# Turning the maxima of a unit as f16, in the step and the bank of the sums

## The chip, the cores and the metric

The kernel runs on one core of one Trainium2 chip. The metric is the device time of one launch in microseconds (us). A core has TensorE (PE; weight loads are shown as PEld), VectorE (DVE), ScalarE (ACT), GpSimd (POOL) and SyncE (SP, which issues most DMAs here). The time before is 2743.02 us, the median of three runs from 2740.77 to 2745.37.

## What is computed

One layer of a bidirectional encoder on two sequences of 2048 tokens, each token 1024 wide, with the same weights. Cut to what matters here:

```python
u = rmsnorm(h, g_norm)
q, k, v, ga, f, gf = split(u @ w_in)              # 8 q heads, 2 kv heads of 64; gates; Fourier input
q, k = rope(rmsnorm(q, g_q)), rope(rmsnorm(k, g_k))
s  = einsum('bkgqd,bskd->bkgqs', qblk, k) * 64 ** -0.5      # 128 queries at a time
pr = softmax(s, axis=-1)
a  = einsum('bkgqs,bskd->bqkgd', pr, v) * silu(ga)
fo = real(fft2(f)) @ w_fmix * silu(gf)
h  = h + concat([a, fo]) @ w_out
h  = h + (p @ w_ple) * sigmoid(rmsnorm(h, g_ple) @ w_ple_gate)
y  = rmsnorm(h, g_final)
```

The change concerns the softmax alone: the maximum of each query's scores, which is taken off before the exponential.

## The kernel before

The program has three stretches. The first, to about 844 us, projects both sequences (`project`). The second, to about 2668 us, is attention; between its steps one filling generator puts work of the other branch into the same engines' queues: first the Fourier branch (`fourier2`), then the output projections (`outp`). What is left of the filling work runs last.

**Units and steps.** Attention has 64 units; a unit is a sequence, a kv head and 128 queries of that head's four q heads. Step `g` belongs to unit `u = g // 8` and block `j = g % 8` of its keys. In a step `scores(u, j)` (L1141) multiplies two half-arrays of keys by the queries into two banks of `ps_s`, ScalarE takes the exponentials `p` (L1144), and GpSimd adds them up into `acc` (L1147, L1149, L1151). The score products stand transposed, keys on partitions, queries along columns. In steps 0 and 4 ("heavy" ones) TensorE multiplies four blocks of `p` by V (`pv`, L1205) and no filling work follows; in the other steps `interleave` draws some, by shares that are fixed in the program.

**Maxima.** A query's maximum has to be known before its first exponential, so each unit's scores are computed once more ahead of time, with queries on partitions: `lead(g)` runs eight pieces `maxima(v, k)` (L1168, two half-array f16 products into the only buffer of `ps_m`, and a row maximum on VectorE, L1176), `AHEAD` = 13 steps before `g`. After the last piece L1181 makes `m4`, [128 queries, 4 heads]. `negate` (L1186, ScalarE) writes it, negated and scaled by 2^-12, twice into a zeroed f32 tile `nm` of 128 x 128. `max_rows` (L1191) turns it: a product with the identity puts the queries along the columns, into 128 columns of a bank of PSUM. L1193 (VectorE) multiplies that by `own`, which leaves each head's row at its place, and writes the f16 tile `mr`; the first product of the next unit's step 0 adds `mr` to the scores with the weights `kone` (2^12).

**The order around it.** PE, ACT, DVE and SP work in the order in which the program issues. With `AHEAD` = 13 and `g = 8u + j`, the last piece of unit u+1 comes in step j = 2, the first of unit u+2 in j = 3, `negate(u+1)` in j = 4 and `max_rows(u+1)` in j = 6, behind that step's maxima. In step 4 `sums(u-1)` (L1237) multiplies `acc` by ones into 256 columns of a bank and `divide` (L1244, L1245, VectorE) takes the reciprocal in place and scales unit u-1's output. `run_slow` then issues one of the long second halves of a split (L1383, L1527) or a final scaling (L1513), two of them in step 0. `load_q` (L1127) loads the queries of unit u+2 at j = 0.

**Banks.** `bank()` gives out banks of PSUM: during the Fourier branch in turn from `ps_g` (two) and `ps_f` (one); once the output projection has begun (`self.grouped`), from the one bank of `ps_f` alone. It is asked for the turn, for the sums and for the embedding products of the filling work (L445 into `ps_f`, read by L1421 and L1423 on VectorE).

**The first unit.** Before attention there are no steps: `leads()` runs the first 13 pieces of `lead` inside the projection's sweeps, one at a time, with the two-bank form of `maxima` in `ps_x`, and `max_rows(0)` behind the piece of g = -2. What is left of them is drained near the end of the projection (L823).

Of the kernel before, what the change touches and what calls it, by code (L numbers as in the profile page):

```python
# [10 lines left out]
F32 = mybir.dt.float32  # L11
F16 = mybir.dt.float16
I32 = mybir.dt.int32
AF = mybir.ActivationFunctionType
ALU = mybir.AluOpType
# [13 lines left out]

CAP = 5.0  # L30
FILL = 765.0
AHEAD = 13
PVG = 4
NBF = 5
NW = 16
# [105 lines left out]
class Build:  # L141
# [957 lines left out]
    def attention(self, kvp):  # L1099
# [3 lines left out]
        nc, st = self.nc, self.st  # L1103
        units = self.unit_order()
        n = len(units)
# [82 lines left out]

        def max_rows(u, ps):

            nc.tensor.matmul(ps, nm[:], self.ident[:], start=True, stop=True)  # L1191
            MR[u] = mr = kvp.tile([128, 4, 128], F16, name="mr", bufs=1)
            nc.vector.tensor_tensor(out=mr[:], in0=ps.unsqueeze(1).to_broadcast([128, 4, 128]),  # L1193
                                    in1=own[:].unsqueeze(2).to_broadcast([128, 4, 128]), op=ALU.mult)

        def pv(u, j0):
            s, kv, t = units[u]
# [56 lines left out]
        for kv in range(2):  # L1254
            load_kv(0, kv)
            load_q(kv)
        nm = kvp.tile([128, 128], F32, name="nm", bufs=1)
        nc.gpsimd.memset(nm[:], 0.0)
        kone = kvp.tile([128, 128], F16, name="kone", bufs=1)
        nc.gpsimd.memset(kone[:], K_ONE)  # L1260
# [11 lines left out]
        def leads():  # L1272
            for g in range(-AHEAD, 0):
                yield from lead(g)
                yield
                if g == -2:
                    max_rows(0, self.bank()[:, 0:128])

        self.ahead = leads()
        pool = yield 0.0  # L1280
# [3 lines left out]
        for g in range(8 * n + 7):  # L1284
            self.step = g
            self.flush()
            u, j = g // 8, g % 8
            if j == 0 and 0 <= u and u + 2 < n:
                load_q(u + 2)
            if j == 4 and u - 1 in fresh:  # L1290
                load_kv(1, fresh[u - 1])
            if 0 <= u < n:
                scores(u, j)
            self.drain(lead(g))
            if j == 4 and 0 <= u - 1 < n:
                ps = self.bank()
                sums(u - 1, ps[:, 0:256])
                divide(u - 1, ps[:, 0:256])
            heavy = (g - 1) % PVG == PVG - 1 and 0 <= g - 1 < 8 * n
            if heavy:  # L1300
                self.run_slow(2 if j == 0 else 1)
                pv((g - 1) // 8, (g - 1) % 8 - PVG + 1)
            if j == 6 and u + 1 < n:
                max_rows(u + 1, self.bank()[:, 0:128])
            yield 0 if heavy else RATE if g >= 8 * n // 2 else 1 if g > FIRST else SLOW


# [547 lines left out]
```

## Time and profile before

| | |
|---|---|
| runs, median | 2743.02 us |
| profiled execution | 2747.83 us, span 2746.0 us |
| granted TensorE clock, mean | 0.991 |
| PE busy | 2649.2 us (96%) |
| DVE busy | 1702.8 us (62%) |
| POOL busy | 1631.3 us (59%) |
| ACT busy | 1213.0 us (44%) |
| DMA | 296.73 MB, mean 108 GB/s |

The profiled execution is one run with the profiler on; its rows carry all durations below. The span runs from the first to the last instruction. Busy times overlap, and a product's duration on PE holds its way through the array, so products that follow each other overlap too: what a product costs the queue is read from the distance between the starts of its neighbours. In rows of products "64\*128" or "128\*128" is the used part of the array (rows \* columns), and an f32 product shows as two rows.

### The profile page before, as it was taken

The numbers are of one execution on the slowest core, as the hardware profiler recorded it, in microseconds if no ns is written. First come the engines' busy times: TensorE is split into PE (matmuls) and PEld (weight loads), VectorE is DVE, ScalarE is ACT, GpSimd is POOL, SyncE is SP. The second block draws the span as 40 slices with busy tenths as digits, with TensorE's granted clock in tenths as the row PEclk, the third lists the DMA queues.
The fourth block names the chain that finished last, engine by engine and source line by source line (L and its number), as shares of the span: only waits on it lengthen the run. The fifth ranks groups of instructions, "written<-read, shape, count | busy, mean of one in ns | idle before, by whom it ended". The sixth has DMA issues, their size and how long they took to land.

```text
span 2746.0 us, 46196 instructions
## 1 busy us (share of the span) xinstructions
PE 2649.2 (96%) x18176; PEld 1261.7 (46%) x18176; DVE 1702.8 (62%) x2477; ACT 1213.0 (44%) x2047; POOL 1631.3 (59%) x1394
## 2 busy tenths in 40 slices
PE   6899999999998998999999999999999999999998
PEld 3455565655555553444434444344444334444443
DVE  6755555564455775666666666666666667666644
ACT  3434333342224553454544555445545445444442
POOL 1223323242335886777777777777777777777760
PEclk9999999999999999999999999999999999999999
DMA  7567567675427662122222223322222222222223
GB/s 233 144 177 199 163 192 189 180 189 118 140 71 229 215 215 83 45 60 63 74 61 60 55 67 81 88 63 69 56 79 58 64 70 68 58 72 74 58 68 76
DMA packets 418554, 296.73 MB, mean 108 GB/s; under 512 B 259456, under 2 KB 360000, under 8 KB 418336
## 3 DMA queue, kind: packets, MB, share of 16 engines
q1 hardware_dynamic: 405424, 252.01, 35.0%
q0 software_dynamic: 12912, 41.77, 4.2%
q8 instruction: 142, 2.33, 0.4%
q14 instruction: 76, 0.62, 0.1%
HBM read 149.50 MB, written 86.51 MB: 86 GB/s over the span
## 4 chain that ended last, share of the span: by engine, by line
PE 86%; DVE 6%; issue 2%; DMA 2%; ACT 1%; POOL 1%; SPq 0%; DVEq 0%; ACTq 0%; POOLq 0%
PE ps_g L1473 22%; PE ps_o L1205 16%; PE ps_x L445 15%; PE ps_s L1141 13%; PE ps_f L445 6%; PE ps_g L445 6%; PE ps_m L1168 4%; PE ps_f L1237 1%; DVE a_mx L1176 1%; PE ps_f L1191 1%; PE ps_g L1012 1%; PE ps_g L1060 1%; DVE w_mx L312 1%; ACT p L1144 0%; PE ps_x L911 0%
## 5 line engine op out<-in xcount | busy, mean ns | idle before, releaser
L1149 POOL TENSOR_TENSOR acc<-acc,p 128x1024 f32<-128x1024 f32 x384 | 910.7, 2372 | 217.8 <-ACT p L1144 172.7
L1176 DVE TENSOR_REDUCE a_mx<-ps_m 128x1 f32<-128x1024 f32 x499 | 610.1, 1223 | 529.9 <-PE ps_m L1168 520.8
L1144 ACT ACTIVATE p<-ps_s,s_scale 128x512 f32<-128x512 f32 x1024 | 647.2, 683 | 659.1 <-PE ps_s L1141 645.6
L1473 PE MATMUL ps_g<-w_pg,hT 64*128 64x512 f16 x2784 | 494.8, 377 | 5.8 <-DMA hT<-h_hl 5.7
L1205 PE MATMUL ps_o<-p,v 128*64 128x512 f32 x2048 | 466.1, 597 | 0.0
L445 PEld LDWEIGHTS <-uc 128*128 128x128 f16 x3072 | 301.3, 98 | 311.8 <-issue 22.4
L1141 PE MATMUL ps_s<-q,k 64*128 64x512 f16 x3072 | 435.0, 378 | 4.9 <-ACT p L1144 4.8
L1473 PEld LDWEIGHTS <-hT 64*128 64x128 f16 x2784 | 200.2, 94 | 165.3 <-issue 20.7
L1141 PEld LDWEIGHTS <-k 64*128 64x128 f16 x3072 | 149.6, 94 | 250.8 <-issue 128.0
L1473 PE MATMUL ps_g<-w_wo,mh 64*128 64x512 f16 x1440 | 261.6, 378 | 1.4 <-DVE seen L1439 1.4
L1205 PEld LDWEIGHTS ps_o<-p,v 128*64 128x64 f32 x2048 | 141.7, 137 | 257.3 <-issue 248.2
L1473 PE MATMUL ps_g<-w_wo,mT 64*128 64x512 f16 x1440 | 256.7, 377 | 0.6 <-DMA mT<-mh 0.6
L1168 PE MATMUL ps_m<-k,q 64*128 64x512 f16 x998 | 202.3, 377 | 11.4 <-DVE a_mx L1176 9.6
L1147 POOL TENSOR_TENSOR acc<-p,p 128x1024 f32<-128x1024 f32 x64 | 150.7, 2354 | 97.7 <-ACT p L1144 97.0
L445 PEld LDWEIGHTS <-w_ga 128*128 128x128 f16 x1536 | 151.4, 99 | 53.7 <-issue 23.3
L928 POOL DMA_DIRECT2D gfd<-gt x32 | 19.2, 601 | 216.0 <-DVE gt L956 211.1
L1473 PEld LDWEIGHTS <-mh 64*128 64x128 f16 x1440 | 99.3, 94 | 89.6 <-issue 14.5
L1473 PEld LDWEIGHTS <-mT 64*128 64x128 f16 x1440 | 100.6, 94 | 84.6 <-issue 2.3
L1221 ACT ACTIVATE tb<-ps_o,a_scale 64x256 f32<-64x256 f32 x128 | 60.0, 469 | 167.4 <-PE ps_o L1205 166.6
L445 PE MATMUL ps_x<-uc,w_ga 128*128 128x256 f16 x1008 | 115.8, 276 | 6.8 <-ACT ge L913 6.2
L1244 DVE RECIPROCAL ps_f<-ps_f 128x256 f32<-128x256 f32 x61 | 107.1, 1756 | 14.2 <-PE ps_f L1237 14.2
L946 POOL DMA_DIRECT2D agd<-gat x64 | 35.8, 559 | 134.7 <-DVE gat L956 134.5
(331 smaller groups left out, 3404.2 us busy)
## 6 DMA issues: line engine op xcount, KB each, us to landing
q<-qTd SPq DMA_DIRECT2D x256, 64.0 KB, 2.2
ag<-agd SPq DMA_DIRECT2D x64, 256.0 KB, 3.3
out<-h POOLq DMA_DIRECT2D x31, 512.0 KB, 3.0
x<-in_x_prompt SPq DMA_DIRECT2D x16, 512.0 KB, 5.6
w_st<-in_w_out SPq DMA_DIRECT2D x32, 256.0 KB, 4.3
gfd<-gt POOLq DMA_DIRECT2D x32, 256.0 KB, 3.2
gd<-ge POOLq DMA_DIRECT2D x32, 256.0 KB, 3.6
agd<-gat POOLq DMA_DIRECT2D x64, 128.0 KB, 2.4
```

Source lines behind the costliest of these rows:

```text
L445: self.nc.tensor.matmul(ps, lhs(ia, k), rhs(ib, k), start=(i == 0), stop=(i == 3 * ks - 1))
L946: nc.gpsimd.dma_start(self.agd[s][1, r * 128:(r + 1) * 128, c * n:(c + 1) * n], gt[:, :n])
L1141: nc.tensor.matmul(S[u][e][:], w[sl], q[sl].rearrange("p h q -> p (h q)"), start=j == i == 0, stop=i + 1 == len(todo), skip_group_check=True)
L1144: nc.scalar.activation(p[:, e, :], S[u][e][:], AF.Exp, scale=self.sc["s_scale"][:])
L1147: nc.gpsimd.tensor_tensor(out=ACC[u][:], in0=P[u, 0][:], in1=p[:], op=ALU.add)
L1149: nc.gpsimd.tensor_tensor(out=ACC[u][:], in0=ACC[u][:], in1=p[:], op=ALU.add)
L1168: nc.tensor.matmul(ps[c], Q[u][0][sl, h, :], kt[s, kv, half][sl, :, 0, :], start=True, stop=True)
L1176: nc.vector.reduce_max(MX[u][:, h, half, c:c + 1], x, axis=AX.X)
L1205: nc.tensor.matmul(o[64 * e:64 * e + 64, :], vt[s, kv, c // 8][:, c % 8, :], p[:, e, :], start=(j == 0), stop=(j == 7))
L1221: nc.scalar.activation(tb[64 * e:64 * e + 64], ov[64 - 64 * e:128 - 64 * e, e], AF.Copy, scale=self.sc["a_scale"][64 - 64 * e:128 - 64 * e ...
L1244: nc.vector.reciprocal(r, r)
L1473: nc.tensor.matmul(g[0][:], g[1](ia, k)[sl], g[2](ib, k)[sl], start=a, stop=z, skip_group_check=True)
```

## The change

`AHEAD` goes from 13 to 14: each piece of maxima and each `negate` comes one step sooner, so the last piece of unit u+1 is in j = 1, the first of unit u+2 in j = 2 and `negate(u+1)` in j = 3. `nm` becomes an f16 tile, and the identity is copied once into an f16 tile `id16` on GpSimd, so the turn is an f16 product. It leaves step 6 and is issued in step 4 ahead of the sums, into columns 256 to 383 of the bank that the sums take anyway; the multiplication into `mr` follows behind `divide`. `max_rows` returns this multiplication as a function for that purpose. Of the pieces that run inside the projection there is one more.

```diff
-AHEAD = 13
+AHEAD = 14
...
         def max_rows(u, ps):
 
-            nc.tensor.matmul(ps, nm[:], self.ident[:], start=True, stop=True)
+            nc.tensor.matmul(ps, nm[:], id16[:], start=True, stop=True)
             MR[u] = mr = kvp.tile([128, 4, 128], F16, name="mr", bufs=1)
-            nc.vector.tensor_tensor(out=mr[:], in0=ps.unsqueeze(1).to_broadcast([128, 4, 128]),
-                                    in1=own[:].unsqueeze(2).to_broadcast([128, 4, 128]), op=ALU.mult)
+            return lambda: nc.vector.tensor_tensor(out=mr[:], in0=ps.unsqueeze(1).to_broadcast([128, 4, 128]),
+                                                   in1=own[:].unsqueeze(2).to_broadcast([128, 4, 128]), op=ALU.mult)
...
-        nm = kvp.tile([128, 128], F32, name="nm", bufs=1)
+        id16 = kvp.tile([128, 128], F16, name="id16", bufs=1)
+        nc.gpsimd.tensor_copy(id16[:], self.ident[:])
+        nm = kvp.tile([128, 128], F16, name="nm", bufs=1)
...
                 if g == -2:
-                    max_rows(0, self.bank()[:, 0:128])
+                    max_rows(0, self.bank()[:, 0:128])()
...
-            if j == 4 and 0 <= u - 1 < n:
+            if j == 4:
                 ps = self.bank()
-                sums(u - 1, ps[:, 0:256])
-                divide(u - 1, ps[:, 0:256])
+                if u + 1 < n:
+                    turned = max_rows(u + 1, ps[:, 256:384])
+                if u > 0:
+                    sums(u - 1, ps[:, 0:256])
+                    divide(u - 1, ps[:, 0:256])
+                if u + 1 < n:
+                    turned()
             heavy = (g - 1) % PVG == PVG - 1 and 0 <= g - 1 < 8 * n
             if heavy:
-                self.run_slow(2 if j == 0 else 1)
+                self.run_slow(1 if j else 2)
                 pv((g - 1) // 8, (g - 1) % 8 - PVG + 1)
-            if j == 6 and u + 1 < n:
-                max_rows(u + 1, self.bank()[:, 0:128])
```

On TensorE, before, a step 6 in the middle of the program; q and k are tiles of queries and keys, hT and mT the operands of the filling work (in such listings an f32 product is one row and has no row for its weight load):

```order
L1141 MATMUL ps_s<-q_16740,k_7187 128x512
L1168 LDWEIGHTS q_17320
L1168 MATMUL ps_m<-k_17145,q_17320 128x512
L1168 LDWEIGHTS q_17320
L1168 MATMUL ps_m<-k_17145,q_17320 128x512
L1191 MATMUL ps_f<-ident,nm 128x128
L1473 LDWEIGHTS mT
L1473 MATMUL ps_g<-w_wo_8663,mT 128x512
L1473 LDWEIGHTS hT
L1473 MATMUL ps_g<-w_pg_9864,hT 128x512
```

There the turn stands between half-array maxima and half-array filling work. On TensorE, now, a step 4 in the middle of the program:

```order
L1141 MATMUL ps_s<-q_16721,k_7187 128x512
L1168 LDWEIGHTS q_17299
L1168 MATMUL ps_m<-k_17123,q_17299 128x512
L1168 LDWEIGHTS q_17299
L1168 MATMUL ps_m<-k_17123,q_17299 128x512
L1191 LDWEIGHTS nm
L1191 MATMUL ps_f<-id_7200,nm 128x128
L1237 MATMUL ps_f<-acc,ones 64x256 x2
L1205 MATMUL ps_o<-p_17305,v_7190 64x512 x2
```

The turn, with a weight load of its own as f16, has moved between the maxima and the sums. On VectorE, before, from the end of a step 3 (the eviction L1421, L1423 of an embedding product) to step 6; L1527 is the second half of a split:

```order
L1421 SCALAR_TENSOR_TENSOR ps_f<-th,ps_f 128x512
L1423 SCALAR_TENSOR_TENSOR h<-ps_f,p_wp_6899,h 128x512
L1176 TENSOR_REDUCE a_mx<-ps_m 128x1 x2
L1244 RECIPROCAL ps_f<-ps_f 128x256
L1245 TENSOR_TENSOR at<-at,ps_f 128x256
L1527 SCALAR_TENSOR_TENSOR h_hl<-h,h_r,h_hl 128x1024
L1176 TENSOR_REDUCE a_mx<-ps_m 128x1 x2
L1193 TENSOR_TENSOR mr<-ps_f,own 128x512
L1176 TENSOR_REDUCE a_mx<-ps_m 128x1
```

Now, the same place (line numbers behind L1258 are up to five higher: L1426, L1428 and L1532 are L1421, L1423 and L1527 of before):

```order
L1426 SCALAR_TENSOR_TENSOR ps_f<-th,ps_f 128x512
L1428 SCALAR_TENSOR_TENSOR h<-ps_f,p_wp_6899,h 128x512
L1176 TENSOR_REDUCE a_mx<-ps_m 128x1 x2
L1244 RECIPROCAL ps_f<-ps_f 128x256
L1245 TENSOR_TENSOR at<-at,ps_f 128x256
L1193 TENSOR_TENSOR mr<-ps_f,own 128x512
L1532 SCALAR_TENSOR_TENSOR h_hl<-h,h_r,h_hl 128x1024
L1176 TENSOR_REDUCE a_mx<-ps_m 128x1 x3
```

The multiplication has moved from behind step 6's maximum to ahead of the split's second half and of step 5's maximum. The other instructions of TensorE, VectorE and ScalarE keep their order, and SP's is unchanged.

## Rows read from the trace of the kernel before

**Rows 1.** The page of the profile: busy time of each engine with its share of the span and its instructions; then the chain of work that ended last, as shares of the span by engine.

```profile
PE 2649.2 (96%) x18176; PEld 1261.7 (46%) x18176; DVE 1702.8 (62%) x2477; ACT 1213.0 (44%) x2047; POOL 1631.3 (59%) x1394
...
PE 86%; DVE 6%; issue 2%; DMA 2%; ACT 1%; POOL 1%; SPq 0%; DVEq 0%; ACTq 0%; POOLq 0%
```

**Rows 2.** Busy time in two windows of the span (window and its length; busy us of PE, PEld, DVE, ACT and POOL, each with its count; granted clock; DMA share; GB/s).

```profile
857.00:1110.00 253.00, 238.48 (x1656) 128.24 (x1658) 162.81 (x199) 128.72 (x213) 189.06 (x134) 0.96 0.57 181
1110.00:2668.00 1558.00, 1539.53 (x11470) 634.67 (x11468) 1004.24 (x1030) 768.11 (x1278) 1161.53 (x969) 1.00 0.25 66
```

**Rows 3.** All of TensorE's waits from 1110 to 2668 us (who waited for whom: us in total, times, longest).

```profile
PE ps_m L1168 <- DVE a_mx L1176: 6.1, 9, 1.2
PE ps_f L445 <- DVE mr L1193: 6.0, 5, 1.5
PE ps_f L1191 <- DVE h L1423: 4.0, 6, 0.7
PE ps_s L1141 <- ACT p L1144: 2.0, 9, 0.3
```

**Rows 4.** The turn's line from 1110 to 2668 us on PE: duration in ns (min/median/max), first and last start.

```profile
L1191 PE MATMUL ps_f<-ident,nm x110: 275/326/377, 1116.5 to 2626.9; 128*128 128x128 f32 x110
```

**Rows 5.** TensorE in order of time (start us, length us, engine, line, operation, out<-in, count): first the maxima and the filling work of a step 5, then the scores, maxima, turn and filling work of the step 6 behind it.

```profile
1712.06 0.38 PE L1168 MATMUL ps_m<-k,q 64*128 64x512 f16 x2
1712.28 0.38 PE L1473 MATMUL ps_g<-w_wo,mh 64*128 64x512 f16 x1
...
1714.22 0.81 PE L1141 MATMUL ps_s<-q,k 64*128 64x512 f16 x6
1714.87 0.38 PE L1168 MATMUL ps_m<-k,q 64*128 64x512 f16 x2
1715.18 0.49 PE L1191 MATMUL ps_f<-ident,nm 128*128 128x128 f32 x2
1715.60 0.39 PE L1473 MATMUL ps_g<-w_wo,mT 64*128 64x512 f16 x1
```

**Rows 6.** TensorE, a step 6 in which the turn waited for its bank (in brackets the idle time and what ended it).

```profile
1553.45 0.38 PE L1168 MATMUL ps_m<-k,q 64*128 64x512 f16 x2
1554.50 0.49 PE L1191 MATMUL ps_f<-ident,nm 128*128 128x128 f32 x2 [0.67 <-DVE h L1423]
1554.92 1.47 PE L1473 MATMUL ps_g<-w_wo,mT 64*128 64x512 f16 x12
```

**Rows 7.** TensorE beside the Fourier branch: maxima and the next product in a step 6, with its turn between them (not shown), and in the step 7 behind it, without one.

```profile
874.73 0.38 PE L1168 MATMUL ps_m<-k,q 64*128 64x512 f16 x2
...
875.36 1.06 PE L1012 MATMUL ps_g<-bd,fT 128*128 128x128 f32 x8
...
877.91 0.38 PE L1168 MATMUL ps_m<-k,q 64*128 64x512 f16 x2
878.22 1.16 PE L1012 MATMUL ps_f<-bd,fT 128*128 128x128 f32 x8
```

**Rows 8.** TensorE, the step 4 of the same unit: maxima and sums.

```profile
1707.05 0.40 PE L1168 MATMUL ps_m<-k,q 64*128 64x512 f16 x2
1707.39 0.65 PE L1237 MATMUL ps_f<-acc,ones 128*64 128x256 f32 x4
```

**Rows 9.** TensorE in the projection: 24 f16 products of 256 columns in the full array, and what follows them.

```profile
808.82 2.78 PE L445 MATMUL ps_x<-wr_kv,uc 128*128 128x256 f16 x24
811.43 0.81 PE L445 MATMUL ps_x<-w_f,uc 128*128 128x512 f16 x3
```

**Rows 10.** VectorE in that unit: the second half of a split behind the reciprocal of step 4, the maximum of step 5, and the multiplication of step 6.

```profile
1710.76 1.70 DVE L1527 SCALAR_TENSOR_TENSOR h_hl<-h,h_r,h_hl 128x1024 f16<-128x1024 f32 x1
1712.49 1.22 DVE L1176 TENSOR_REDUCE a_mx<-ps_m 128x1 f32<-128x1024 f32 x1
...
1716.43 0.68 DVE L1193 TENSOR_TENSOR mr<-ps_f,own 128x512 f16<-128x512 f32 x1
```

**Rows 11.** The closest place: VectorE's maximum of a step 5, and TensorE's maxima of the step 6 behind it.

```profile
1739.90 1.21 DVE L1176 TENSOR_REDUCE a_mx<-ps_m 128x1 f32<-128x1024 f32 x1
...
1741.47 0.57 PE L1168 MATMUL ps_m<-k,q 64*128 64x512 f16 x2
```

**Rows 12.** ScalarE, the exponentials of step 3 of that unit, and the negation behind those of step 4.

```profile
1705.12 1.26 ACT L1144 ACTIVATE p<-ps_s,s_scale 128x512 f32<-128x512 f32 x2 [1.11 <-PE ps_s L1141]
...
1708.45 0.22 ACT L1186 ACTIVATE nm<-a_m 128x8 f32<-128x8 f32 x1
```

**Rows 13.** SP's four loads of q of one unit, the maxima of that unit's step 2 on TensorE, and the time from issue to landing over all 256 such loads.

```profile
1233.44 2.47 SPq L1127 DMA_DIRECT2D q<-qTd  x4
...
1239.74 0.39 PE L1168 MATMUL ps_m<-k,q 64*128 64x512 f16 x2 [0.52 <-DVE a_mx L1176]
...
DMA to landing us min/median/max: 2.0/2.2/5.7
```

**Rows 14.** The start of attention: an instruction of VectorE's rotation of keys, SP's first loads of q in attention, and TensorE's two waits for them.

```profile
824.88 2.30 DVE L732 CAST ks<-kd 128x256 f16<-128x256 f32 x1
...
851.84 2.40 SPq L1127 DMA_DIRECT2D q<-qTd  x4
...
854.38 0.67 PE L1168 MATMUL ps_m<-k,q 64*128 64x512 f16 x2 [1.68 <-DMA q<-qTd]
857.81 3.75 PE L1060 MATMUL ps_g<-c,g_in 128*128 128x128 f32 x16 [2.77 <-DMA g_in<-gd]
```

## The prediction, made before the changed kernel had run

> **What bounds the kernel now.** I read the page first: TensorE is busy for 96% of the span, and the chain that ended last runs over it for 86% [rows 1]. A busy share is only an average, so the windows come next. From 1110 to 2668 us, where attention runs beside the output projection, TensorE is busy for 1539.5 of 1558 us at a granted clock of 1.00 (the 2.4 GHz level), and no other engine passes 1161.5 us (GpSimd) [rows 2]. The list of TensorE's waits in that stretch has four rows and 18.1 us in all; two of them, 10.0 us, name the turn of the maxima (L1191) or its multiplication (L1193) [rows 3]. So in this stretch a microsecond taken from TensorE's queue is a microsecond of the kernel, unless another engine then comes late. This stretch holds 55 of the 64 units, eight steps each; a step is scores, maxima, then (steps 0 and 4) the products with V, or else filling work.
>
> **What the turn costs now.** The f32 turn is two matmul rows, 110 rows for 55 units [rows 4]. Its price isn't its duration, since matmuls overlap, but the distance between its neighbours. In step 5 the filling work starts 0.22 us after the maxima; in step 6, with the turn between them, 0.73 us [rows 5]. So a turn costs 0.51 us, and 55 of them 28.0 us.
>
> Six turns also wait for the one bank of ps_f that the filling work's eviction (L1423) still reads: there the distance is 1.47 us [rows 6], so 0.74 us over the 0.73, and 6 x 0.74 = 4.4 us. The reverse wait, a filling product in ps_f that waits for L1193, is the row of 6.0 us, the longest 1.5 [rows 3]. Both kinds go: between step 4 and the next step 4 nothing of the maxima holds that bank any more. Together 28.0 + 4.4 + 6.0 = 38.4 us.
>
> The eight units before 1110 us gain less: the neighbour there is a full-array f32 product, and the distance is 0.63 us with a turn and 0.31 us without [rows 7], so 0.32 us, at most 2.6 us for eight. TensorE has 14.5 us of idle time there [rows 2], so I take half, 1.3 us (0 to 2.6).
>
> **What the turn costs in its new place.** It stands between the maxima and the sums of step 4, which today start 0.34 us after the maxima [rows 8]. Those 0.34 us already hold the change from half of the array to all of it (0.22 would be the distance between half-array products), so the turn pays that change and the sums don't pay it again. Left is one f16 weight load and 128 columns. No row shows such a product. From below: a 256-column f16 product follows the one before it after 0.109 us (24 from 808.82 to 811.43) [rows 9], and half the columns make 0.055. From above: the f32 turn between the maxima and a full-array product, 0.32 us [rows 7], since half the rows can't cost more. I take 0.11, the stream's distance as it stands: it is the nearer row in type and array, and it holds a weight load of the same size for each product. For 63 units: 6.9 us (3.5 to 20).
>
> On the passes: the two rows per f32 product are what the Trainium skill ("FP8 and Floating Point Precision", TensorE Precision Notes) describes from the other side, four passes for a true f32 product. By passes and columns alone I would count 3 x 128 columns at 2.4 GHz, 0.16 us per unit, 10 us in all. The rows say 0.51 us; the sum goes by them.
>
> **What follows the move on VectorE.** The multiplication (0.68 us [rows 10]) leaves step 6 and goes into step 4 behind the reciprocal and its product. Queued behind it are the second half of a split (L1527, L1383) and then the maximum of step 5 (L1176), for which TensorE waits at the maxima of step 6, as ps_m has one buffer. Today the split ends at 1712.46 and the maximum starts at 1712.49, so it will be late by 0.68 + 0.03 - 0.11 = 0.60 us against TensorE (which gets 0.11 later itself). It ends at 1713.71 and TensorE comes for the bank at 1714.87 [rows 5, 10]: 1.16 us of slack, so no wait. The closest place I found has 0.36 us: maximum to 1741.11, maxima at 1741.47 [rows 11]; it would wait 0.24. Going through all units in this way I get 1.1 us; I take 1 (0 to 55 x 0.24 = 13).
>
> **Is the operand there?** The negation (L1186, 0.22 us) moves from behind the exponentials of step 4 to behind those of step 3, so only one step is left before the turn instead of two. The exponentials of step 3 end at 1706.38 (started 1705.12, 1.26 long) [rows 12], the negation would end at 1706.60, and the turn would start where the sums do now, 1707.39 [rows 8]. 0.79 us remain, and this unit is among the tightest, since a step's scores wait for the exponentials before them. Behind the waiting turn stand the sums and 16 products with V; the wait costs nothing as long as that margin holds.
>
> **Is q there?** All first maxima come one step sooner: those of unit u+2 in step 2, while its four q loads are issued at step 0 in unchanged order on SP. The tightest place of the long stretch: issued 1233.44 to 1235.91, 2.2 us to landing (median), so 1238.1; step 2's maxima start at 1239.74 [rows 13]. 1.6 us remain there. At the start it is short: unit 2's q is issued from 851.84, the maxima of step 3 wait until 854.38 already, and now those of step 2 will. But the filling work waits until 857.81 for g_in from the same queue [rows 14], and step 3's scores and maxima take 0.65 + 0.22 us [rows 5], so nothing is lost.
>
> **Before attention.** The first of 14 first-maxima steps is added inside the projection, and the first turn and one pair of maxima move into its last drain. On VectorE they stand just before the rotation of keys around L732 at 824.88 [rows 14]: one multiplication of 0.68 us and two row maxima of 512 columns, 1.2 us by the one of 1024, so 1.9 us ahead of the keys on whose transposes the loads at 851.84 wait. That L732 takes 2.30 us for a cast of 256 columns, much of it evidently held up by something else, so part of the delay may vanish in it. I take 1 us (0 to 2). The copy of the identity on GpSimd is one instruction beside the projection: nothing.
>
> **Sum.** 38.4 + 1.3 - 6.9 - 1 - 1 = 30.8 us less. The profiled execution took 2747.83 us (span 2746.0), 4.8 above the median of the runs, so it would come to 2717; against the median, 2743.0 - 30.8 = 2712.
>
> **Rivals.**
>
> *The setup moves along (chance 0.11).* Weight loads in the full array may not hide around a lone product, and the turn costs 0.32 us in step 4 too. For it: the distance of 0.32 was measured between just such neighbours [rows 7]. Against it: that product is two rows and this one a single row [rows 4]. Time: 38.4 + 1.3 - 20.2 - 2 = 17.5, so 2726. The Trainium skill ("TensorE: Matmul & The Clock Gate", Part 3, The mechanism) speaks for it: weight loads overlap running products only where the row groups differ, which full-array products never do. By that rule this rival would be the forecast; the trace disagrees with the rule in the stream of 0.109 us.
>
> *VectorE becomes the bound in steps 4 to 6 (0.06).* If no slack were left, each unit would wait the whole 0.60 us in step 6: 63 x 0.60 = 37.8, and 30.8 + 1 - 37.8 = -6: 2749, slower. It turns slower from a mean wait of 0.5 us per unit. For it: a second half of a split of 1.70 us stands right behind the moved multiplication [rows 10]. Against it: 1.16 us of slack in a usual unit.
>
> *q comes late (0.02).* If its landing slipped until every unit waited 1 us in step 2, 62 us: 2774. The margin says no.
>
> *Nothing changes (0.04).* If a slower engine sets the pace and TensorE's busy time is only modelled: 2743. Against it: the next busiest, GpSimd, works 75% of the stretch, and no wait of TensorE's there names it [rows 2, 3].
>
> **How the numbers follow.** The forecast, 2712, has 0.77; its own range is 2704 to 2722, from the bounds of the turn (3.5 to 10, the upper third left to the rival), the eight early units and the two terms of 1. Taking in the first rival the range is 2703 to 2730, beyond which lie the rest of the VectorE case, late q and no change. No change means within 0.2%, 5.5 us, about what this measurement can tell. Faster: 0.77 + 0.11 + a third of the VectorE case = 0.90. Same: 0.04 + a third of it = 0.06. Slower: 0.04.
>
> **What would show it.** Right: L1191 has half the rows, all in step 4, and the filling work follows step 6's maxima after 0.22 us; the rows of L1423 before L1191 and of L1193 before L445 are gone from TensorE's waits; the sums start about 0.45 us after step 4's maxima. Wrong: a wait of L1168 for L1176 in step 6 or for q in step 2 that grows by tens of us, a wait of L1191 for the negation, or the sums at 0.65 us and more.

## The result, and the profile after

The changed kernel took 2719.48 us (median of four runs, 2718.41 to 2721.44) beside 2744.19 us of the kernel before (four runs, 2740.77 to 2747.75): a ratio of 0.991, 95% interval 0.9898 to 0.9922, 24.7 us less. The forecast was 2712 us, 30.8 us less. The kernel is faster, inside the range given (2703 to 2730) and in the forecast's own range (2704 to 2722), and 7.5 us above the forecast itself.

The page's line of busy times, and one window of the changed kernel (columns as in [rows 2]):

```profile
PE 2628.8 (97%) x18112; PEld 1257.7 (46%) x18112; DVE 1698.0 (62%) x2478; ACT 1212.0 (45%) x2047; POOL 1634.7 (60%) x1395
```

```profile
1110.00:2668.00 1558.00, 1545.81 (x11527) 643.53 (x11526) 1015.28 (x1056) 774.47 (x1285) 1167.01 (x981) 1.00 0.26 68
```

TensorE is as busy as before in that window, at the same clock of 1.00 [rows 2]; the profiled execution ends sooner (span 2717.9 us, execution 2719.65) because there is less for it to do. Its waits from 1110 to 2668 us, now:

```profile
PE ps_m L1168 <- DVE a_mx L1176: 8.2, 9, 1.7
PE ps_s L1141 <- ACT p L1144: 2.0, 9, 0.3
PE ps_g L1478 <- DVE mh L1388: 1.6, 1, 1.6
PE ps_g L1478 <- DVE h L1404: 0.4, 2, 0.2
```

Both rows that named the turn, 10.0 us [rows 3], are gone. In their place are 2.1 us more for the maxima (8.2 against 6.1) and two short new rows, 2.0 us. The turn's form, for the 57 turns into ps_f (it is one matmul row per unit now, [rows 4] had two):

```profile
L1191 PE MATMUL ps_f<-id,nm x57: 229/230/230, 1039.5 to 2591.9; 128*128 128x128 f16 x57
```

TensorE in a step 4, and the maxima and first filling work of the step 6 behind it:

```profile
1694.40 0.41 PE L1168 MATMUL ps_m<-k,q 64*128 64x512 f16 x2
1694.74 0.23 PE L1191 MATMUL ps_f<-id,nm 128*128 128x128 f16 x1
1694.90 0.65 PE L1237 MATMUL ps_f<-acc,ones 128*64 128x256 f32 x4
...
1702.38 0.38 PE L1168 MATMUL ps_m<-k,q 64*128 64x512 f16 x2
1702.60 0.38 PE L1478 MATMUL ps_g<-w_wo,mT 64*128 64x512 f16 x1
```

In step 6 the filling work follows the maxima after 0.22 us, where it was 0.73 [rows 5]. In step 4 the sums follow the maxima after 0.50 us by this pair of rows (the median over 53 units of the long stretch, from the exact starts, is 0.468), where it was 0.34 [rows 8] (median 0.306). So the turn costs 0.162 us in its new place, not 0.11.

**Where the time went, step by step.** I use one measure for all runs: the *long stretch*, from the first scores of unit 9 to the last scores of unit 63, by the starts in each trace. Before it lasts 1534.1 us (1121.5 to 2655.6), after 1509.7 us (1117.7 to 2627.4): 24.4 us less. Added up over its units by the step:

| step of a unit | before | after | difference |
|---|---|---|---|
| 6 | 198.3 us | 160.6 us | -37.7 |
| 7 | 154.0 us | 154.9 us | +0.9 |
| 4 | 287.1 us | 296.0 us | +8.9 |
| 0, 1, 2, 3, 5 | 894.7 us | 898.2 us | +3.5 |

(The table's steps add up to the stretch but for roundings.) The stretch holds 54 turns, since unit 63 has no next unit to prepare: 54 x 0.162 = 8.7 of the 8.9 us of step 4. The two traces lie 28.1 us apart in span; the other 3.7 us lie ahead of unit 9, where traces of one kernel differ by 2 to 3 us (below).

### The profile page after: what moved, and what is told of

Same layout as the page of the kernel before. It is cut to its first block, busy times and chain, and to the rows that moved or that the text cites. A ratio compares the mean times of both kernels' runs of the same rounds, so it can differ in the third digit from the quotient of the medians.

```text
span 2717.9 us, 46091 instructions
## 1 busy us (share of the span) xinstructions
PE 2628.8 (97%) x18112; PEld 1257.7 (46%) x18112; DVE 1698.0 (62%) x2478; ACT 1212.0 (45%) x2047; POOL 1634.7 (60%) x1395
## 4 chain that ended last, share of the span: by engine, by line
PE 81%; DVE 7%; issue 5%; DMA 3%; POOL 2%; ACT 1%; SPq 0%; DVEq 0%; POOLq 0%; ACTq 0%
PE ps_g L1478 22%; PE ps_o L1205 15%; PE ps_s L1141 13%; PE ps_x L445 12%; PE ps_f L445 6%; PE ps_g L445 5%; PE ps_m L1168 4%; PE ps_f L1237 1%; DVE a_mx L1176 1%; DVE t L703 1%; PE ps_g L1012 1%; PE ps_g L1060 1%; DMA gd<-ge 1%; POOL t L707 1%; DMA w_st<-in_w_ple_gate 1%
## 5 line engine op out<-in xcount | busy, mean ns | idle before, releaser
L1149 POOL TENSOR_TENSOR acc<-acc,p 128x1024 f32<-128x1024 f32 x384 | 918.5, 2392 | 207.2 <-ACT p L1144 170.4
```

Source lines behind the costliest of these rows:

```text
L1149: nc.gpsimd.tensor_tensor(out=ACC[u][:], in0=ACC[u][:], in1=p[:], op=ALU.add)
```

## The experiments

All runs in one table. Each ratio is to the runs of before on the same chip in the same batch (medians 2747.22, 2747.85 and 2747.63 us in the three batches: e1 to e4, e5 to e8, e9 to e12); the first two rows are those of the result. The times in the expectations were counted from the first result's 2744, so some 3 us of each difference in time are the batch; the long stretch is free of that.

| kernel | median us | ratio to before, 95% interval | long stretch, us |
|---|---|---|---|
| before | 2744.19 | | 1534.1 |
| after | 2719.48 | 0.991 (0.9898 to 0.9922) | 1509.7 |
| e1: f16 turn alone | 2736.88 | 0.9963 (0.9948 to 0.9978) | 1525.2 |
| e2: move alone, f32 | 2740.11 | 0.9975 (0.9966 to 0.9985) | 1524.1 |
| e3: two f16 turns | 2727.02 | 0.9927 (0.9912 to 0.9942) | 1515.4 |
| e4: turn behind the sums | 2731.25 | 0.994 (0.9924 to 0.9957) | 1519.0 |
| e5: turn in two column halves | 2715.47 | 0.9882 (0.9867 to 0.9896) | 1506.2 |
| e6: after, again | 2722.08 | 0.9903 (0.9887 to 0.992) | 1510.0 |
| e7: before, again | 2750.49 (one run) | | 1533.9 |
| e8: a bank of its own | 2875.29 (one run) | | 1657.0 |
| e9: multiplication three times | 2736.11 | 0.9957 (0.994 to 0.9973) | 1525.4 |
| e10: multiplication last | 2722.61 | 0.9913 (0.9898 to 0.9928) | 1509.9 |
| e11: e5 and e10 | 2717.32 | 0.9892 (0.9877 to 0.9907) | 1505.0 |
| e12: AHEAD 14 alone | 2745.69 | 0.9991 (0.9981 to 1.0) | 1535.0 |

### e6 and e7: both kernels again

> The changed kernel once more, on the chip of this call, since the kernel before was 3 us slower in the last call than in the first result. Expected: 24 to 29 us less than before here, as its two traces differ by 28; 1509 to 1511 us from the scores of unit 9 to the last scores.

> The kernel before once more, for a second trace of it. If the stretch that the change is about is steady, the time from the scores of unit 9 to the last scores is 1534 us within 1, and what sets its runs apart (2741 to 2751 us so far) lies ahead of it, in the projection and the Fourier units, where the granted clock is not 1.00 throughout.

The long stretch repeats within 0.3 us for both kernels, so a difference of one us in it means something. What varies lies ahead of it: unit 9 began at 1121.5 and 1124.3 us in the two traces of before, at 1117.7 and 1119.9 in those of after, and between 1117.0 and 1126.0 over all traces, in no order that follows the edits. So the long stretch (24.4 and, in this pair, 23.9 us) is what the edit gives; the difference of the medians, 24.7 us in the first result and 25.8 us here, agrees with it within the spread of the runs.

### e1: the f16 turn alone

```diff
-        nm = kvp.tile([128, 128], F32, name="nm", bufs=1)
+        id16 = kvp.tile([128, 128], F16, name="id16", bufs=1)
+        nc.gpsimd.tensor_copy(id16[:], self.ident[:])
+        nm = kvp.tile([128, 128], F16, name="nm", bufs=1)
...
-            nc.tensor.matmul(ps, nm[:], self.ident[:], start=True, stop=True)
+            nc.tensor.matmul(ps, nm[:], id16[:], start=True, stop=True)
```

> The f16 turn alone: the turn stays in step 6 with a bank of its own, AHEAD stays 13. Theory A (a turn's price is the distance that it adds between its neighbours, and most of that is weight loads which a lone full-array product leaves open): the maxima are followed by the turn after 0.31 us, as the f32 turn is, and the turn by the half-array filling work after 0.16 us, as the sums follow the f16 turn in the changed kernel; that is 0.47 instead of 0.73 us, 0.26 x 55 = 14 us less, 1 us more beside the Fourier branch; both bank waits of before (10 us) stay. About 2729 us. Theory B (the f32 turn's price is its three extra passes over 128 columns at 2.4 GHz, nothing else is saved): 0.16 x 63 = 10 us less, 2734 us. Theory C (what costs is the place between half-array products, not the type): no more than 3 us less, 2741 us or above.

TensorE's turn and what follows it: first beside the Fourier branch, where full-array products follow, then in a step 6 of the long stretch:

```profile
931.31 0.23 PE L1191 MATMUL ps_g<-id,nm 128*128 128x128 f16 x1
931.37 1.11 PE L1012 MATMUL ps_f<-bd,fT 128*128 128x128 f32 x8
...
1712.87 0.38 PE L1168 MATMUL ps_m<-k,q 64*128 64x512 f16 x2
1713.18 0.23 PE L1191 MATMUL ps_f<-id,nm 128*128 128x128 f16 x1
1713.34 0.39 PE L1475 MATMUL ps_g<-w_wo,mT 64*128 64x512 f16 x1
```

The distances are those of theory A: 0.31 and 0.16 us, 0.47 in all, 0.26 less than the f32 turn's 0.73 [rows 5]. The time is 2736.88, not 2729: of the 14 us that 54 turns make, the long stretch keeps 8.9. Two waits grew, and they hold nearly all of the rest (2.7 and 1.9 us more than in [rows 3]):

```profile
PE ps_f L445 <- DVE mr L1193: 8.7, 9, 1.8
PE ps_m L1168 <- DVE a_mx L1176: 8.0, 10, 1.4
```

The new observation is in the rows at 931 us: where the turn is followed by a product in the whole array, that one starts 0.06 us after it, not 0.16.

### e2: the move alone

```diff
-        id16 = kvp.tile([128, 128], F16, name="id16", bufs=1)
-        nc.gpsimd.tensor_copy(id16[:], self.ident[:])
-        nm = kvp.tile([128, 128], F16, name="nm", bufs=1)
+        nm = kvp.tile([128, 128], F32, name="nm", bufs=1)
...
-            nc.tensor.matmul(ps, nm[:], id16[:], start=True, stop=True)
+            nc.tensor.matmul(ps, nm[:], self.ident[:], start=True, stop=True)
```

(against the changed kernel)

> The move alone: the changed kernel with nm and the identity in f32. Theory A: step 6 gains as in the changed kernel (38 us), and the turn's two rows between the maxima and the sums cost 0.31 + 0.21 + 0.11 to 0.21 - 0.31 = 0.32 to 0.42 us a unit, 20 to 26 us: 12 to 18 us less than before, 2726 to 2732 us. Theory B (passes alone): the turn costs 0.16 us more per unit than the f16 one, 10 us, 2729.5 us. Theory C (the place is what counts, the type is nothing): as the changed kernel, 2719 to 2722 us.

```profile
1705.18 0.41 PE L1168 MATMUL ps_m<-k,q 64*128 64x512 f16 x2
1705.52 0.49 PE L1191 MATMUL ps_f<-ident,nm 128*128 128x128 f32 x2
1705.94 0.65 PE L1237 MATMUL ps_f<-acc,ones 128*64 128x256 f32 x4
```

From the maxima to the sums the median is 0.724 us, so the f32 turn costs 0.418 us in step 4: the upper end of theory A. Passes alone (B) and the place alone (C) are both out. The time, 2740.11, is 8 us above A's range, 5 with the batch allowed for: by 63 x 0.418 = 26.3 us the gain of 38.4 shrinks to 12, and this trace too has longer waits for the maxima (8.9 us). The long stretch is 10.0 us shorter than before.

e1 and e2 together separate the change's two halves. From f32 to f16 saves 0.257 us per turn in step 6 (0.727 to 0.470) and 0.256 in step 4 (0.724 to 0.468): the same in both places, 14 us for 54 turns. The move saves 0.096 us per unit in the turn itself (0.258 to 0.162), 5 us, and the 10 us of bank waits.

### e3: two turns in step 4

```diff
                     turned = max_rows(u + 1, ps[:, 256:384])
+                    nc.tensor.matmul(ps[:, 384:512], nm[:], id16[:], start=True, stop=True)
```

> The changed kernel with the f16 turn of step 4 issued twice, the second into columns 384 to 511 of the same bank, which nothing reads. Theory A (the 0.16 us between turn and sums is the weight load of the sums, which 128 columns can't cover): the second turn follows the first after 0.09 to 0.11 us, its own weight load, and the sums follow it after 0.16 us as before: 6 to 7 us more, 2726 us. Theory D (0.16 us is what any such lone product costs): 0.16 us again, 10 us more, 2729.5 us. Theory E (the 128 columns alone): 0.05 us, 3.4 us more, 2723 us.

```profile
1695.59 0.40 PE L1168 MATMUL ps_m<-k,q 64*128 64x512 f16 x2
1695.92 0.23 PE L1191 MATMUL ps_f<-id,nm 128*128 128x128 f16 x1
1695.99 0.22 PE L1301 MATMUL ps_f<-id,nm 128*128 128x128 f16 x1
1696.14 0.65 PE L1237 MATMUL ps_f<-acc,ones 128*64 128x256 f32 x4
```

The second turn starts 0.066 us after the first (median), and the sums 0.149 us after the second. It costs 0.056 us a unit, which is theory E's price and neither A's nor D's: 128 columns and hardly anything else. The time, 2727.02, would suit A too, but not for A's reason: of 5.7 us more in the long stretch step 4 holds 3.0 (299.0 against 296.0), and the waits for the maxima grew by 2.3 (10.5 us). So neither a weight load nor a lone product as such makes up the 0.16 us; it is what stands behind the turn that makes it. The weight loads of the second turn and of the sums, beside these rows, show where the time goes:

```profile
1695.93 0.10 PEld L1301 LDWEIGHTS <-nm 128*128 128x128 f16 x1
1696.13 0.20 PEld L1237 LDWEIGHTS ps_f<-acc,ones 128*64 128x64 f32 x4
```

The second turn's load starts right behind the first turn's start, 0.056 us ahead of its own product; the sums' load starts 0.002 us ahead of theirs (medians).

### e4: the turn behind the sums

```diff
-                if u + 1 < n:
-                    turned = max_rows(u + 1, ps[:, 256:384])
                 if u > 0:
                     sums(u - 1, ps[:, 0:256])
+                if u + 1 < n:
+                    turned = max_rows(u + 1, ps[:, 256:384])
+                if u > 0:
                     divide(u - 1, ps[:, 0:256])
```

> The changed kernel with the turn between the sums and the products with V instead of ahead of the sums; on VectorE nothing moves. The sums then follow the maxima after 0.31 us as before the change, and the products with V followed the sums after 0.21 us. Theory A (the price is the open weight load of what follows the turn, and the products with V have weights as wide as the sums'): 0.15 to 0.2 us more between sums and products with V than without a turn, so the same time within 3 us, 2717 to 2722 us. Theory F (each change between the column halves of the sums and the full array costs a load of its own): 0.25 us or more, 6 us slower than the changed kernel or worse, 2725 us or above.

```profile
1702.85 0.65 PE L1237 MATMUL ps_f<-acc,ones 128*64 128x256 f32 x4
1703.44 0.23 PE L1191 MATMUL ps_f<-id,nm 128*128 128x128 f16 x1
1703.60 3.65 PE L1205 MATMUL ps_o<-p,v 128*64 128x512 f32 x16
```

From the last row of the sums the turn starts after 0.312 us (median), the products with V after another 0.160; without a turn it was 0.209 in all. Two products on either side, both in column halves (128\*64), and the lone whole-array product between them pays going and coming back: step 4 is 313 ns longer than without a turn, against 162 in the changed kernel. Of the 313, 262 lie between the sums and the products with V; the other 51 lie within these products, and why is open. Theory F; 2731.25 us.

**Theory G**, from these four. Of how the array is divided there are three kinds here: row halves (64\*128: scores, maxima, half of the filling work), the whole (128\*128: the turn, the embedding products, the Fourier branch) and column halves (128\*64: sums, products with V). A product of 128 columns costs some 0.06 us among its own kind. Each change of kind costs 0.094 to 0.103 us more: 0.307 against 0.212 behind the maxima, 0.160 against 0.066 behind the turn, 0.312 against 0.209 behind the sums, and 0.525 against 0.429 from the products with V back to the scores. The rows of PEld add what happens there. At all 388 changes of kind in the changed kernel's long stretch the next weight load starts 1 to 5 ns ahead of its product; where the line changes and the kind stays, it starts 15 ns ahead or more, 214 by the median. So at a change no load runs ahead, and the 0.095 us have passed before the load starts. What the engine waits for in them no run shows.

### e5: the turn in the kind of the sums

```diff
-            nc.tensor.matmul(ps, nm[:], id16[:], start=True, stop=True)
+            for e in range(2):
+                sl = slice(64 * e, 64 * e + 64)
+                nc.tensor.matmul(ps[sl], nm[:, sl], id16[:], start=True, stop=True)
```

> The changed kernel with the turn as two products of 64 weight columns each, side by side in the two column halves, as the sums and the products with V behind it are. Theory G (from the first four experiments: a product of 128 columns costs 0.066 us in a stream, and each change between row halves, whole array and column halves about 0.095 us; the maxima work in row halves, the whole-array turn adds one change, this one adds none): turn to sums 0.066 us instead of 0.160, 0.094 x 63 = 6 us less than the changed kernel of this call, about 2713 to 2716 us, faster than both. Theory A' (the price is an open weight load of the f32 sums whatever stands before them): 0.15 us or more again, and the time of the changed kernel, or 3 to 6 us more if the two halves' loads add up.

```profile
1694.14 0.25 PE L1193 MATMUL ps_f<-id,nm 128*64 128x128 f16 x2
1694.22 0.60 PE L1239 MATMUL ps_f<-acc,ones 128*64 128x256 f32 x4
```

The same sums by twice as many products, and cheaper: the two halves start 3 ns apart, the sums 0.077 us behind the second, and step 4 as a whole is only 29 ns longer than without any turn (the sums themselves take less behind it). The halves' weights are also half as wide, but the change behind the maxima costs the same 0.306 us, and the sums' load now starts 53 ns ahead of them, as inside a kind. 2715.47 us against 2722.08 for the changed kernel in the same batch: 6.6 us less, in the range of theory G, and faster than both kernels. That the time is in the range is in part luck: the long stretch is 3.8 us shorter (1506.2 against 1510.0 in e6), 7.3 less in step 4 and 3.5 more elsewhere, with waits for the maxima 3.2 us longer (11.5 against 8.3). By 133 ns a unit the whole would have been 8.4.

### e8: a bank for the turn

```diff
-                ps = self.bank()
                 if u + 1 < n:
-                    turned = max_rows(u + 1, ps[:, 256:384])
+                    max_rows(u + 1, self.bank()[:, 0:128])()
                 if u > 0:
+                    ps = self.bank()
                     sums(u - 1, ps[:, 0:256])
                     divide(u - 1, ps[:, 0:256])
-                if u + 1 < n:
-                    turned()
```

> The changed kernel, but the turn takes a bank of its own, and the multiplication stands behind it, ahead of sums and division: in the long stretch bank() has one bank, so the sums wait until the multiplication has read the turn. If sharing the bank is what spares TensorE a wait in step 4: the sums wait 0.23 (way of the product) + 0.68 (multiplication) + some 0.1 for each of 55 units, 45 to 60 us, and the kernel is slower than before, about 2765 to 2780 us. If the bank plays no part: 2717 to 2722 us.

The sign was right and the size far off: 1657.0 us in the long stretch, 147 more than the changed kernel. TensorE in one step 4, then VectorE beside it, then TensorE's window behind the wait:

```profile
1704.45 0.23 PE L1191 MATMUL ps_f<-id,nm 128*128 128x128 f16 x1
1706.53 0.65 PE L1237 MATMUL ps_f<-acc,ones 128*64 128x256 f32 x4 [1.84 <-DVE mr L1193]
1706.98 5.33 PE L1205 MATMUL ps_o<-p,v 128*64 128x512 f32 x16
```

```profile
1704.56 1.23 DVE L1176 TENSOR_REDUCE a_mx<-ps_m 128x1 f32<-128x1024 f32 x1 [1.58 <-PE ps_m L1168]
1705.70 0.68 DVE L1193 TENSOR_TENSOR mr<-ps_f,own 128x512 f16<-128x512 f32 x1
```

```profile
1707.00:1712.20 5.20, 5.20 (x18) 1.72 (x14) 3.38 (x3) 0.00 (x0) 1.08 (x1) 0.67 0.07 13
```

I had left out what stands ahead of the multiplication in VectorE's queue: the maximum of step 4, 1.23 us. So TensorE waits 1.84 us, not one. And behind the wait the 16 products with V take 5.33 us instead of some 3.60, at a granted clock of 0.67 over that window: part of it at the 1.2 GHz level, and TensorE had stood idle for 1.84 us just before. That doesn't happen each time: the sums wait 1.8 to 2.1 us in 53 units, and in 29 of them the products with V take 4.8 to 6.6 us until the next scores, in the other 24 the usual 3.6. The mean clock of the long stretch is 0.97 here, and 1.00 in both kernels. Of the 147 us, the way from the maxima to the sums makes 104 and the products with V 44, added up over the units. Sharing the bank of the sums, with the multiplication behind the division, is thus what spares TensorE this wait where bank() has a single bank.

### e9 and e10: the multiplication on VectorE

```diff
                 if u + 1 < n:
-                    turned()
+                    for _ in range(3):
+                        turned()
```

> The changed kernel with the multiplication into mr issued three times in a row in step 4, 1.37 us more on VectorE ahead of the split's second half and the maximum of step 5. Theory V (VectorE has slack there: in the changed kernel the maxima of step 6 come a median 1.1 us after step 5's maximum has ended, by its trace; a split that starts later also meets less of GpSimd's addition): going through the 53 units of the long stretch in the changed kernel's trace, with the split's second half lasting 1.27 us or until 1.08 us after the end of the addition it meets, I get 11 us more, so 2731 to 2735 us. Rival (VectorE has no slack left in steps 4 to 6): 1.37 x 63 = 86 us more, 2806 us.

2736.11 us: 15.7 us more in the long stretch than the changed kernel, somewhat over the 11 us worked out from its trace, and nowhere near 86. Step 6 holds 15.0 of the 15.7 us. VectorE has slack for one multiplication in step 4, not for three; the changed kernel's own waits for the maxima have none in step 6, where I had looked for them, and of e9's nineteen, eleven stand there:

```profile
PE ps_m L1168 <- DVE a_mx L1176: 16.9, 19, 1.6
```

e10 only moves the multiplication:

```diff
-                if u + 1 < n:
-                    turned()
...
                 pv((g - 1) // 8, (g - 1) % 8 - PVG + 1)
+            if j == 4 and u + 1 < n:
+                turned()
```

> The changed kernel with the multiplication behind the long second half of a split in step 4 instead of ahead of it; both stay ahead of step 5's maximum. If the length of the second halves depends on when they meet GpSimd's addition: they start 0.68 us sooner and are as long as before the change again (medians 1.40 us for L1383 and 1.68 us for L1527, against 1.28 us in the changed kernel), the one wait of 1.6 us for mh is gone, and the waits for a_mx are near 6 us as before the change, not 8: 2 to 4 us less than the changed kernel, 2716 to 2720 us. If the length has nothing to do with it: medians stay at 1.28 us, and the time at 2719 to 2722 us.

The second halves of one kind of split on VectorE, from 1110 to 2668 us (min/median/max in ns): in the kernel before, in the changed one, and in e10.

```profile
L1527 DVE SCALAR_TENSOR_TENSOR h_hl<-h,h_r,h_hl x28: 1274/1702/3299, 1124.5 to 2631.4; 128x1024 f16<-128x1024 f32 x28
```

```profile
L1532 DVE SCALAR_TENSOR_TENSOR h_hl<-h,h_r,h_hl x30: 1274/1277/2798, 1120.7 to 2664.8; 128x1024 f16<-128x1024 f32 x30
```

```profile
L1532 DVE SCALAR_TENSOR_TENSOR h_hl<-h,h_r,h_hl x29: 1275/1660/3435, 1124.2 to 2652.3; 128x1024 f16<-128x1024 f32 x29
```

Those of the other kind (mh) have medians of 1.45, 1.28 and 1.41 us. The lengths go with the moment at which the instruction starts, as expected, and the wait for mh is gone. The time isn't less: 1509.9 us in the long stretch, and waits for the maxima of 9.3 us instead of the 6 that I expected. e11 repeats it on top of e5:

> The turn in two column halves and the multiplication behind the second half of the split, together. If the two are independent: 6 us and up to 4 us less than the changed kernel, 2710 to 2716 us; if the multiplication's place gives nothing, the 2715.5 us of the two halves alone.

2717.32 us and 1505.0 us: 1.2 us less than e5 in the long stretch, while the median of the runs is 1.9 us higher, so no gain is shown. The multiplication's place on VectorE is worth nothing beside the whole-array turn and 1 us at most beside the two halves.

### e12: AHEAD at 14 alone

```diff
-AHEAD = 13
+AHEAD = 14
```

> The kernel before with AHEAD at 14 and nothing else: the maxima and the negation come a step sooner, the f32 turn stays in step 6. My forecast took 1 us of loss for this at the start of attention (0 to 2), behind a longer rotation of keys. If that is right, the scores of unit 0 start 1 us later than before, and the time is 0 to 2 us longer; if the delay vanishes in the waits that are there, both are the same within 1 us. If q, now asked for a step sooner, came late all through, tens of us more.

2745.69 us, a ratio of 0.9991 (0.9981 to 1.0); the scores of unit 0 start at 843.9 us in its trace and the long stretch takes 1535.0, 1.0 us more than in the two traces of before, with waits for the maxima of 7.2 us instead of 5.6 to 6.1. No loss at the start is to be seen, and no late q.

## Why the prediction was right or wrong

**Removed from step 6: right.** Forecast were 28.0 us for the turn and 10.4 for both waits, 38.4; steps 6 and 7 of the long stretch are 36.8 us shorter. The distance went from 0.73 to 0.22 us, and both rows of waits are gone, as the prediction's last part asked.

**The turn in its new place: the step that failed.** I argued that "the turn pays that change and the sums don't pay it again", and took 0.11 us. The turn does pay the change from row halves to the whole array (0.308, as the sums paid 0.306 before). But the sums work in column halves, so they pay another one behind it. The row had it: [rows 8] says 128\*64 for the sums, and I read it as "all of the array". The term was 63 x 0.11 = 6.9 us and measured 63 x 0.162 = 10.2, just above the forecast's own bound for it (10). e3 (a second whole-array turn for 0.056), e4 (a turn between two groups in column halves for 0.313) and e5 (a turn in column halves for 0.029) tell this apart from a price of the type, the lone product or the load as such.

**The first rival**, that the turn's setup moves along at 0.32 us and the time is 2726, was wrong: 0.162 is nearer to 0.11 than to 0.32. That the time, 2719.48, lies midway between 2712 and 2726 says nothing for it, since the other terms fell short as well (the balance below). The Trainium skill's rule for it ("TensorE: Matmul & The Clock Gate", Part 3, The mechanism: loads overlap running products only in other row groups) doesn't hold inside one kind, where the second turn of e3 came 0.066 us after the first in the same rows. At a change of kind no load runs ahead, which the rule would give; but the sums use the same rows as the second turn, so it is the kind that decides here and not the rows.

**VectorE, forecast as 1 us in step 6: wrong place.** No wait in step 6 came. I had the second half of the split start 0.68 us later and last as long as before. It started later and was shorter: 1.28 us instead of 1.70 in the unit of [rows 10].

```profile
1698.72 1.28 DVE L1532 SCALAR_TENSOR_TENSOR h_hl<-h,h_r,h_hl 128x1024 f16<-128x1024 f32 x1
1700.00 1.23 DVE L1176 TENSOR_REDUCE a_mx<-ps_m 128x1 f32<-128x1024 f32 x1
```

This maximum ends 1.15 us before TensorE's maxima at 1702.38, and it was 1.16 before the change: the slack is as it was. Instead some 4 us came elsewhere: 2.1 us more for the maxima, in steps 2, 3, 4 and 7, and 2.0 us in the two new rows, of which 1.6 stand in one place (below). e10 removes the 1.6 us and gets nothing for it. The runs put the waits for the maxima at 5.6 to 11.5 us in one order or another of nearly the same instructions (e9 apart); which of them comes is left open.

**The start: 1 us forecast, none found.** The multiplication and two maxima do stand ahead of the rotation of keys now. VectorE there, in the kernel before and in the changed one:

```profile
824.42 0.42 DVE L731 TENSOR_TENSOR kd<-kd,ks 128x256 f32<-128x256 f32 x1
...
827.21 2.52 DVE L733 TENSOR_TENSOR kd<-kd,ks 128x256 f32<-128x256 f32 x1
...
830.53 1.21 DVE L735 TENSOR_TENSOR qs<-t,qs 128x1024 f16<-128x1024 f32 x1
```

```profile
824.63 1.28 DVE L1176 TENSOR_REDUCE a_mx<-ps_x 128x1 f32<-128x512 f32 x2
825.83 1.05 DVE L731 TENSOR_TENSOR kd<-kd,ks 128x256 f32<-128x256 f32 x1
...
829.27 0.83 DVE L733 TENSOR_TENSOR kd<-kd,ks 128x256 f32<-128x256 f32 x1
...
830.48 1.22 DVE L735 TENSOR_TENSOR qs<-t,qs 128x1024 f16<-128x1024 f32 x1
```

L731 starts 1.4 us later, L735 no later at all: L733 takes 0.83 us instead of 2.52. The delay vanished in time that was lost already. On TensorE the wait for q grew and the one for g_in shrank by nearly as much, which the prediction had said would cost nothing [rows 14]:

```profile
854.31 0.85 PE L1168 MATMUL ps_m<-k,q 64*128 64x512 f16 x2 [4.60 <-DMA q<-qTd]
...
857.68 3.75 PE L1060 MATMUL ps_g<-c,g_in 128*128 128x128 f32 x16 [0.60 <-DMA g_in<-gd]
```

**The operand and q: right.** No row of TensorE's waits names the negation, or q in the long stretch.

**The early units**, forecast as 1.3 us of gain, can't be told from what differs between traces there.

**The balance**, for the long stretch and its 54 turns (the forecast counted 55): forecast 37.9 - 54 x 0.11 - 1 = 31.0 us, measured 24.4. Of the 6.6 between them the turn's price in step 4 is 3.0 (8.9 instead of 5.9), the removal 1.1 (36.8 instead of 37.9), and other steps 2.5 (3.5 instead of 1).

**The range.** The bounds that the prediction names for its own range (the turn at 3.5 to 10, the eight early units, the two terms of 1, each from 0 to 2) add up to 2705.5 to 2718.6, not to 2704 to 2722. The result is in the range as stated and 0.9 us above that sum: the turn alone came out at its upper bound, and VectorE's waits elsewhere had no term.

## What to carry to other kernels

Price a moved matmul by both of its neighbours, and by how each of the three divides the array: here the turn lengthened its step by 0.03 us among its own kind, by 0.16 between two other kinds and by 0.31 as a foreigner between two alike. Where a small product can be written in its neighbours' kind, write it so, even if it takes twice as many instructions. And when an instruction joins an engine's queue, list what stands ahead of it as well as what waits behind: e8 lost 147 us where the multiplication and a maximum ahead of it stood in TensorE's way.

## What was not expected of the hardware

**VectorE's instruction ends 1.08 us after GpSimd's.** The second half of a split reads two arrays of SBUF. It takes 1.27 us alone; where it meets one of GpSimd's additions under way (L1149) it lasts longer. GpSimd in the kernel before, and in the changed one at two places, with VectorE at the second:

```profile
1704.16 7.22 POOL L1149 TENSOR_TENSOR acc<-acc,p 128x1024 f32<-128x1024 f32 x3 [0.99 <-ACT p L1144]
```

```profile
1693.95 4.80 POOL L1149 TENSOR_TENSOR acc<-acc,p 128x1024 f32<-128x1024 f32 x2
...
2114.38 4.79 POOL L1149 TENSOR_TENSOR acc<-acc,p 128x1024 f32<-128x1024 f32 x2
```

```profile
2117.04 3.21 DVE L1388 SCALAR_TENSOR_TENSOR mh<-ag,mix_s,mh 128x1024 f16<-128x1024 f32 x1
```

Before, the additions end at 1704.16 + 7.22 = 1711.38 and the split of [rows 10] at 1712.46, 1.08 us later. At 2117 the additions end at 2119.17 and the split at 2120.25, 1.08 us later again, and this is the 1.6 us wait for mh:

```profile
2120.31 0.39 PE L1478 MATMUL ps_g<-w_wo,mh 64*128 64x512 f16 x1 [1.59 <-DVE mh L1388]
```

It is so in all fourteen traces: every second half in the window 1110 to 2668 us that took 1.3 us or more, 458 in all, ends 1.08 to 1.09 us after an instruction of GpSimd. The other way round it holds as well: of 107 additions that start while a second half is under way, 105 end 2.20 to 2.23 us after it, and an addition takes 2.34 us at the least.

In the unit shown above the split starts at 1698.72, when the additions end (1698.75), and takes 1.28 us. So pushing this instruction back by some 0.6 us can save 0.4 us, or cost 1.9 where it meets the next addition. The instructions with an operand in PSUM don't show it: L1193 took 0.68 us in every unit. The Trainium skill says so ("SBUF — State Buffer", SBUF: two separate sides): VectorE with two SBUF inputs and GpSimd take turns on one pair of ports, each for a whole instruction. These rows agree, but for how long the loser still needs, which they add.

**A change of how the array is divided costs about 0.095 us**, in each direction measured, and no weight load runs ahead of it (theory G). And **waits of 1.8 to 2.1 us on TensorE were followed by a lower clock** in 29 of 53 units (e8), which made 44 of the 147 us that e8 lost.
